# RWKV's normalisation moved from the end of the kernel into the second half of its chain

## The chip, the cores and the metric

The kernel runs on one core of one Trainium2 chip. Times are device microseconds (us) of one execution. A core has TensorE (PE in the rows, its weight loads PEld), VectorE (DVE), ScalarE (ACT), GpSimd (POOL) and SyncE (SP), which issues nearly all DMAs. Each engine works through its own list of instructions in order.

## The reference, cut to what matters

One layer takes 2048 latent and 256 context tokens of width 1024. After a projection one half of the heads does RWKV-7 time mixing in both directions, the other half latent attention:

```
S = S*w + (S@a) b + v k        y = S@r            (forward and backward)
y  = y_f + y_b
yn = (y - mean) * rsqrt(var + 64e-5) * lnx_g + lnx_b        (per head of 64)
rw = (yn + bonus) * silu(gate),   bonus = sum(r*(k_f+k_b)*r_k) * v
mla = softmax(q k^T) v * silu(gate)            (8 heads, 2304 keys)
out = rms_norm(x + gate * (concat(rw, mla) @ w_out))
```

## The kernel before, in words

`phase_in` projects (to about 960 us of the span), `qkv` makes queries, keys and values (to about 1207 us), then `attention` runs. It has 16 jobs (4 pairs of heads, 4 blocks of 512 queries), each of 9 macro steps; a macro step scores two key tiles for two heads (L1425 to L1427, three fp32r products each), exponentiates on ScalarE (L1429), sums the denominators on GpSimd (L1434), and multiplies by V (L1452). Between the scores PE makes the next job's row maxima (L1306), which VectorE reduces (L1307); both share three PSUM banks (`bs`) with the scores.

RWKV works on 36 chunks of 64 tokens, forward and backward at once, and rides along: a chunk n takes three macro steps, called thirds here: m = 0 (`chain1`, `scores` of chunk n+2, `chain1b`), m = 1 (`chain2`), m = 2 (`chain3`, `chain4`, `scores` of n+3). `slot` is called five times in a macro step and gives a stage of the chunkwise inverse (`inverse`, a generator) and `transposed`. `load_bk` issues the load of x and its scaling (L247 to L253). 18 macro steps of the chain run in `qkv`, the next 99 in jobs 0 to 10. `inverse` masks the 128 x 1024 matrix `ph` three times per chunk on VectorE (L343) and spreads results into block-diagonal tiles, one direction by a ScalarE, one by a VectorE copy (L348). `chain4` writes each direction's y to DRAM (L466).

When the chain is done, `post` prepares the output weights and then, for 16 tiles of 128 tokens, loads both y, sums and normalises them on VectorE (L1546 to L1571), transposes on PE (L1578), gates, splits into high and low parts and writes `s_mix`. `out_tiles` loads `s_mix` and multiplies by the weights (L1609), adds the residual and normalises. `late` hands out steps of `post`, and then of `out_tiles`, one quarter of the tokens at a time, between the macro steps. A quarter can start when the last pair of heads is done with it, and in the kernel before only when all of `post` is done.

The order on PE is that of the code; on the other engines a scheduler sets it within the dependencies.

Of the kernel before, what the change touches and what calls it, by code (L numbers as in the profile page):

```python
# [8 lines left out]
F32 = mybir.dt.float32  # L9
# [130 lines left out]
class Rwkv:  # L140
# [3 lines left out]
    def __init__(self, kern, es):  # L144
# [4 lines left out]
        self.total = 3 * (NC + 3)  # L149
# [9 lines left out]
        lvl = st_.tile([P, 4, P], F16, name="lvl")  # L159
# [13 lines left out]
        nc.gpsimd.memset(self.E, 1.0)  # L173
        lo_, up_ = slice(0, 64), slice(64, 128)
# [21 lines left out]
    def slot(self, g):  # L196

        k, j = divmod(g, 5)
        n, m = divmod(k, 3)
        n -= 3  # L200
        if m == 1 and j == 2:
            if 0 <= n + 2 < self.NC:
                self.transposed(n + 2)
            if 0 <= n + 3 < self.NC:
                self.load_bk(n + 3)
        for p in list(self.inv):
            if g - 15 * (p + 1) - 7 in self.STAGES:
                if next(self.inv[p], None) is None:
                    del self.inv[p]

    def tiled(self, k, between=None):
# [5 lines left out]
        if m == 0:  # L217
# [65 lines left out]
    def transposed(self, n):  # L283
# [3 lines left out]
        for d in range(2):  # L287
# [4 lines left out]
            nc.scalar.copy(t, ps)  # L292
# [27 lines left out]
    def inverse(self, n):  # L320
# [20 lines left out]
        def masked(i):  # L341
            pm = op.tile([P, 8, P], F16, name=f"pm{par}")
            nc.vector.tensor_tensor(pm, ph, self.lv8(i), op=ALU.mult)  # L343
            return pm

        def spread(name, x):
            for d, ur, vr in self.dirs:
                (nc.vector.tensor_copy if d else nc.scalar.copy)(self.bd[name][ur, :, ur], x[ur])  # L348
            return self.bd[name]

        pm = masked(0)
        T = None
        yield 1
        for i in range(3):
# [38 lines left out]
        Rf = s["R"] = op.tile([P, 8, 64], F32, name="Rf", bufs=2)  # L393
# [16 lines left out]
    def chain1b(self, n):  # L410
# [11 lines left out]
        if self.full(n):  # L422
            y = s["y"] = self.op.tile([P, 512], F32, name="y")
# [30 lines left out]
    def chain4(self, n):  # L454
# [9 lines left out]
        nc.vector.tensor_tensor(y, ps, y, op=ALU.add)  # L464
        for (d, ur, vr), c in zip(self.dirs, self.chunks[n]):
            nc.sync.dma_start(self.k.s_y[d, c * 64:c * 64 + 64], y[vr])  # L466


class Kern:
# [37 lines left out]
    def load_consts(self):  # L507
# [7 lines left out]
        self.blk = c.tile([P, P], F32, name="blk")  # L515
# [3 lines left out]
    def vectors(self, raw):  # L519
# [4 lines left out]
        self.vec = c.tile([P, NV], F32, name="vec")  # L524
# [711 lines left out]
    def late(self, rest):  # L1236
# [10 lines left out]
        self.pc += (34 + 11 * (L // P)) / (self.POST_T * rest)  # L1247
# [4 lines left out]
    POST_T = 0.75  # L1252
# [3 lines left out]
    RW_QKV = 18  # L1256

# [64 lines left out]
    def attention(self, top, es, right, k, q, load_q, maxima, sets, pieces):  # L1322
# [77 lines left out]
        for ji, (hp, qt) in enumerate(jobs):  # L1400
# [10 lines left out]
            rate = 2 * NQS * NT / max(1, 4 * (NM - 2)) + 8  # L1411
            for m in range(NM):
                if k < rw.total:
                    rw.begin(k)
                elif self.post_ is None:
                    right.close()
# [4 lines left out]
                for j in range(4):  # L1421
# [13 lines left out]
                    if 1 <= m < NM - 1:  # L1435
                        due += rate
# [30 lines left out]
        while k < rw.total:  # L1467
# [4 lines left out]
            k += 1  # L1472
        if self.post_ is None:
# [8 lines left out]
    def post(self, es):  # L1482
# [32 lines left out]

# [5 lines left out]
        h64 = lambda t: t.rearrange("p (h i) -> p h i", i=64)  # L1521
# [15 lines left out]
        V = nc.vector  # L1537
        D1 = []
        nx = load(0)
        for tt in range(NTL + 2):  # L1540
            cur, nx = nx, load(tt + 1)
            if cur:

                ya, vg = cur
                y, y2, vt = h64(ya[:, 0]), h64(ya[:, 1]), h64(vg[:, 0])
                V.tensor_tensor(y, y, y2, op=ALU.add)  # L1546
                yield 1
                st = sp.tile([P, 2, 8], F32, name="st", bufs=3)
# [143 lines left out]
```

## Time and profile before

| | us |
|---|---|
| median of 3 runs (lowest, highest) | 3057.66 (3046.7, 3091.68) |
| profiled execution | 3088.95 |
| its span | 3087.2 |
| PE / DVE / POOL / ACT busy | 2757.4 / 1852.2 / 1407.5 / 1320.9 |
| mean granted TensorE clock | 0.931 |

The page cuts the span into 40 slices of 77 us; jobs 0 to 10 (with the chain) fill slices 17 to 32, jobs 11 to 15 the rest. The clock is given as a share of 2.4 GHz; it has two levels, 1.0 and 0.5 (1.2 GHz), and a value between is a mean over time.

### The profile page before, as it was taken

How to read it: one execution, taken by the hardware profiler on the slowest of the kernel's cores; microseconds unless marked ns; L12 is line 12 of the kernel's file. 1: busy time of each engine (PE TensorE's matmuls, PEld its weight loads, DVE VectorE, ACT ScalarE, POOL GpSimd, SP SyncE). 2: the span in 40 equal slices, each digit the busy share in tenths (PEclk: the TensorE clock that was granted, in tenths of full speed). 3: DMA queues.
4: the chain of work that ended last, by engine and by line, in shares of the span. 5: the costliest groups of instructions: out<-in, count | busy, mean ns of one | idle time of the engine just before them, and what ended most of it. 6: DMA issues, size and time to landing. Idle time of an engine off the chain costs nothing.

```text
span 3087.2 us, 55094 instructions
## 1 busy us (share of the span) xinstructions
PE 2757.4 (89%) x22035; PEld 2081.2 (67%) x22035; DVE 1852.2 (60%) x2867; ACT 1320.9 (43%) x2317; POOL 1407.5 (46%) x1220
## 2 busy tenths in 40 slices
PE   5999999999998898899888888888998977888998
PEld 3997899987787786666666666666666644444776
DVE  3356834266523575777766776775776757997213
ACT  3446744355523433445444444444454442333221
POOL 2323323332332122566555566564665655776332
PEclk7998999999899998999998999998999977898999
DMA  5234542234545776122133222233221144433443
GB/s 195 80 91 125 143 149 88 80 105 121 165 142 174 251 227 157 50 69 70 39 100 89 61 70 60 59 87 88 75 69 49 36 124 128 123 106 116 147 137 116
DMA packets 409466, 336.66 MB, mean 109 GB/s; under 512 B 130598, under 2 KB 341841, under 8 KB 408185
## 3 DMA queue, kind: packets, MB, share of 16 engines
q1 hardware_dynamic: 405775, 327.19, 36.2%
q8 instruction: 173, 2.83, 0.4%
q0 software_dynamic: 992, 3.21, 0.3%
q10 hardware_dynamic: 2442, 2.73, 0.3%
q14 instruction: 84, 0.69, 0.1%
HBM read 210.68 MB, written 122.31 MB: 108 GB/s over the span
## 4 chain that ended last, share of the span: by engine, by line
PE 44%; DVE 14%; DMA 7%; ACT 5%; issue 3%; POOL 1%; SPq 1%; ACTq 0%; POOLq 0%; DVEq 0%
PE bo L1452 7%; PE bx L1609 6%; PE bs L1425 4%; DMA x<-s_x 4%; DVE m L1307 4%; PE pm L117 4%; PE bs L1306 3%; PE bs L1427 3%; PE bs L1426 3%; ACT pt L1429 2%; PE bc L407 2%; PE bx L332 2%; DVE pm L343 2%; DVE x L253 2%; PE bs L1097 2%
## 5 line engine op out<-in xcount | busy, mean ns | idle before, releaser
L1434 POOL TENSOR_TENSOR acc<-acc,pt 128x512 f32<-128x512 f32 x512 | 673.3, 1332 | 612.6 <-ACT pt L1429 608.1
L1429 ACT ACTIVATE pt<-bs 128x512 f32<-128x512 f32 x576 | 342.4, 598 | 574.3 <-PE bs L1427 554.8
L1307 DVE TENSOR_REDUCE m<-bs 128x1 f32<-128x512 f32 (+1 forms) x736 | 401.3, 567 | 187.9 <-PE bs L1306 184.0
L1425 PE MATMUL bs<-q,kt 97*128 97x512 f32 x576 | 282.2, 490 | 44.6 <-ACT pt L1429 22.2
L1452 PE MATMUL bo<-pt,vt 128*64 128x512 f32 x1152 | 310.9, 665 | 0.0
L549 POOL TENSOR_TENSOR wlo<-wraw,whi 128x1024 fp32r<-128x1024 f32 (+1 forms) x56 | 134.3, 2399 | 276.2 <-PE pm L117 177.8
L1427 PE MATMUL bs<-q,kt 97*128 97x512 f32 x576 | 237.9, 413 | 0.0
L1426 PE MATMUL bs<-q,kt 97*128 97x512 f32 x576 | 236.9, 411 | 0.0
L1306 PE MATMUL bs<-kt,q 96*128 96x512 f32 (+1 forms) x480 | 181.9, 408 | 54.3 <-DVE m L1307 18.1
L1425 PEld LDWEIGHTS bs<-q,kt 97*128 97x128 f32 x576 | 112.9, 196 | 125.8 <-ACT pt L1429 39.8
L1306 PEld LDWEIGHTS bs<-kt,q 96*128 96x128 f32 x480 | 91.1, 190 | 120.0 <-ACT pt L1429 43.3
L132 ACT COPY u<-pm 128x342 f32<-128x342 f32 (+1 forms) x168 | 74.1, 441 | 214.7 <-PE pm L117 214.5
L1452 PEld LDWEIGHTS bo<-pt,vt 128*64 128x64 f32 x1152 | 80.3, 153 | 126.8 <-issue 122.1
L1427 PEld LDWEIGHTS bs<-q,kt 97*128 97x128 f32 x576 | 114.1, 198 | 27.3
L1609 PE MATMUL bx<-wohi,big 128*128 128x512 f32 x496 | 126.0, 394 | 3.8 <-DMA big<-s_mix 3.8
L253 DVE TENSOR_TENSOR x<-x 128x512 f32<-128x512 f32 x72 | 65.8, 952 | 99.4 <-ACT x L250 99.3
L1426 PEld LDWEIGHTS bs<-q,kt 97*128 97x128 f32 x576 | 115.1, 200 | 4.6
L978 POOL TENSOR_TENSOR xt<-z,nk 128x512 f32<-128x512 f32 (+1 forms) x40 | 53.1, 1327 | 142.8 <-ACT z L977 80.6
L343 DVE TENSOR_TENSOR pm<-bdph,lvl 128x1024 f16<-128x1024 f16 x108 | 108.0, 1000 | 8.5 <-PE bx L332 5.2
L1609 PEld LDWEIGHTS bx<-wohi,big 128*128 128x128 f32 x496 | 93.7, 190 | 25.0 <-issue 4.8
L1645 DVE TENSOR_TENSOR acc<-bx,big 128x512 f32<-128x512 f32 x32 | 22.0, 690 | 143.3 <-PE bx L1609 137.2
L826 DVE SCALAR_TENSOR_TENSOR kd<-z,u 128x512 f32<-128x512 f32 x32 | 38.9, 1218 | 111.4 <-ACT z L824 111.4
(321 smaller groups left out, 6548.6 us busy)
## 6 DMA issues: line engine op xcount, KB each, us to landing
wraw<-in_w_in SPq DMA_DIRECT2D x54, 512.0 KB
x<-s_x SPq DMA_DIRECT2D x72, 384.0 KB
s_x<-xt SPq DMA_DIRECT2D x32, 512.0 KB
big<-s_mix SPq DMA_DIRECT2D x24, 512.0 KB
s_kn<-hl SPq DMA_DIRECT2D x36, 256.0 KB
ar<-s_nr SPq DMA_DIRECT2D x72, 128.0 KB
uv<-s_v SPq DMA_DIRECT2D x72, 128.0 KB
s_x<-cum SPq DMA_DIRECT2D x32, 256.0 KB
```

Of the source, the lines that this page charges most:

```text
L253: nc.vector.tensor_tensor(self.bk[:, d], self.bk[:, d], cum[:, d].unsqueeze(2).to_broadcast([P, 4, 2, 64]), op=ALU.mult)
L343: nc.vector.tensor_tensor(pm, ph, self.lv8(i), op=ALU.mult)
L549: (eng_lo or nc.vector).tensor_tensor(lo, x, hi.bitcast(F32), op=ALU.subtract)
L1306: nc.tensor.matmul(ps[:, 0:w], q[0:96, e, 0, i * P:(i + 1) * P], ks[e], start=True, stop=True)
L1307: nc.vector.tensor_reduce(m5[:, e * NQS + i, j:j + 1], ps[:, 0:w], axis=AX.X, op=ALU.max)
L1425: nc.tensor.matmul(ps, ks[:, e, 0, sl], q[:, e, 0], start=True, stop=False)
L1426: nc.tensor.matmul(ps, ks[:, e, 0, sl], q[:, e, 1], start=False, stop=False)
L1427: nc.tensor.matmul(ps, ks[:, e, 1, sl], q[:, e, 0], start=False, stop=True)
L1429: nc.scalar.activation(pt, ps, AF.Exp, scale=SCALE)
L1434: nc.gpsimd.tensor_tensor(acc[e], held[e] if kt == 1 else acc[e], pt, op=ALU.add)
L1452: nc.tensor.matmul(oo[64 * e:64 * e + 64], VS[j][:, i, 64 * e:64 * e + 64], pts[kt, e], start=kt == 0, stop=kt == NK - 1)
L1609: nc.tensor.matmul(ps, x[:, i], a[:, k, 512 * h:512 * h + 512], start=n == 0, stop=n == last)
```

## The change

1. `post` loses the RWKV tiles. From chunk `half` = 20 on, where the other direction's y of the same tokens lies in DRAM already, `chain4` starts a generator `normed`: the y of the other direction is loaded (`load_other`), and ten steps, one per slot, do the sum, the normalisation (gain and bias in ScalarE's copy out of PSUM after the transposition), the bonus (GpSimd, transposed too), the gate, the split (low half on GpSimd) and the writes to `s_mix`. Three macro steps are added at the chain's end (`total`). 
2. `inverse` keeps one of its three masks; the other two become a multiplication as the product is spread from PSUM, both directions on VectorE (`level`). Copies of R go to ScalarE. One of two copies in `transposed` goes to VectorE.
3. `load_bk` and `transposed` move from m = 1 to m = 0.
4. The maxima are shared 1.5 : 1 : 0.6 over the thirds in the first half of the chain, evenly after it, and after the chain from the third macro step of a job on.
5. `POST_T` goes from 0.75 to 0.3 with far fewer steps, so that `out_tiles` may start as soon as a quarter is ready, at a lower rate, and waits six steps behind its first load.

```diff
-        self.total = 3 * (NC + 3)
+        self.half = NCC + (NC - NCC) // 2
+        self.total = 3 * (NC + 3) + 3
...
-        if m == 1 and j == 2:
-            if 0 <= n + 2 < self.NC:
-                self.transposed(n + 2)
-            if 0 <= n + 3 < self.NC:
-                self.load_bk(n + 3)
+        if m == 0 and j == 3 and 0 <= n + 2 < self.NC:
+            self.transposed(n + 2)
+        if m != 1 or j == 1:
+            next(self.norm, None)
...
                 self.load_ar(n + 3)
+                self.load_bk(n + 3)
...
                 self.chain2(n)
+                if n >= self.half:
+                    self.load_other(n)
...
-            nc.scalar.copy(t, ps)
+            (nc.vector.tensor_copy if d else nc.scalar.copy)(t, ps)
...
+        def level(name, x, i):
+
+            for d, ur, vr in self.dirs:
+                nc.vector.tensor_tensor(self.bd[name][ur, :, ur], x[ur],
+                                        self.lvl[ur, i, ur].unsqueeze(1).to_broadcast([64, 8, 64]), op=ALU.mult)
...
-                pm = masked(1)
...
-            G = spread(f"g{par}", prod(pm, T))
+            G = level(f"g{par}", prod(ph, T), lev)
...
-                        pm = masked(2)
...
-                        Rb = spread("f", R)
+                        Rb = spread("f", R, both=True)
...
+        if n < self.half:
+            for (d, ur, vr), c in zip(self.dirs, self.chunks[n]):
+                nc.sync.dma_start(self.k.s_y[d, c * 64:c * 64 + 64], y[vr])
+        else:
...
+            self.norm = self.normed(n, s)
...
+            nc.gpsimd.tensor_tensor(h64(vb[vr]), h64(s["uv"][d][vr]), bc(bon[vr, t // P], 64), op=ALU.mult)
+        yield 1
+        V.tensor_tensor(y, y, s["yo"], op=ALU.add)
+        yield 1
...
+        V.tensor_reduce(st[:, 0], h64(y), axis=AX.X, op=ALU.add)
+        V.tensor_scalar(st[:, 0], st[:, 0], 1.0 / 64, None, op0=ALU.mult)
+        yield 1
+        V.tensor_tensor(h64(y), h64(y), bc(st[:, 0], 64), op=ALU.subtract)
+        sq = op.tile([P, 4, 2, 64], F32, name="gt")
+        nc.scalar.activation(flat(sq), y, AF.Square)
+        yield 1
+        V.tensor_reduce(st[:, 1], h64(flat(sq)), axis=AX.X, op=ALU.add)
+        V.tensor_scalar(st[:, 1], st[:, 1], 1.0 / 64, 64e-5, op0=ALU.mult, op1=ALU.add)
+        nc.gpsimd.tensor_tensor(st[:, 0], st[:, 1], self.k.mhalf.to_broadcast([P, 8]), op=ALU.pow)
+        yield 1
+        V.tensor_tensor(h64(y), h64(y), bc(st[:, 0], 64), op=ALU.mult)
...
+        pb = self.k.banks.tile([P, 2, 512], F32, name="bc")
+        for q, x in enumerate((y, vb)):
+            for b in range(4):
+                nc.tensor.transpose(pb[:, q, b * P:(b + 1) * P], x[:, b * P:(b + 1) * P], self.k.ident)
+        for b in range(4):
...
+            nc.scalar.activation(y[:, bs], pb[:, 0, bs], AF.Identity, scale=self.lgb[:, 0, b:b + 1],
...
+        V.tensor_tensor(y, y, pb[:, 1], op=ALU.add)
+        yield 1
+        V.tensor_tensor(y, y, g.rearrange("p b e t -> p (b e t)"), op=ALU.mult)
+        yield 1
...
+        self.k.split(hi, lo, y.rearrange("p (b e t) -> p b e t", e=2, t=64), eng_lo=nc.gpsimd)
+        for q, x in enumerate((hi, lo)):
+            for d, t in enumerate(t0):
+                nc.sync.dma_start(self.k.s_mix[q, 0:4, :, t:t + 64].rearrange("b p t -> p b t"),
...
-    POST_T = 0.75
+    POST_T = 0.3
...
+    MAXIMA = (1.5, 1, 0.6)
...
         nx = self.out_load(qt * nt, nk)
-        yield 1
+        for _ in range(6):
+            yield 1
```

**VectorE at the end of third m = 2 of chunk 25.** `bdg` is the spread product, `st` the state, `y` the output, `sm` the masked scores, `m` the maxima. Before:

```order
L348 CAST bdg_8168<-bx 64x8x64
L370 TENSOR_TENSOR R_22902<-bx,R_22522 128x512
L343 TENSOR_TENSOR pm_23083<-bdph_8160,lvl 128x1024
L348 COPY bdf<-R_22902 64x8x64
L450 TENSOR_TENSOR st_8153<-bx,st_8154 128x512
L452 TENSOR_TENSOR st_8153<-st_8153,gg 128x256 x2
L464 TENSOR_TENSOR y<-bx,y 128x512
L313 TENSOR_TENSOR sm_22955<-bc,mask 128x4x128 x2
```

Now:

```order
L361 TENSOR_TENSOR bdg_8168<-bx,lvl 64x8x64 x2
L384 TENSOR_TENSOR R_22996<-bx,R_22605 128x512
L463 TENSOR_TENSOR st_8153<-bx,st_8154 128x512
L465 TENSOR_TENSOR st_8153<-st_8153,gg 128x256 x2
L477 TENSOR_TENSOR y<-bx,y 128x512
L503 TENSOR_TENSOR y<-y,bt 128x512
L506 TENSOR_REDUCE st<-y 128x8
L507 TENSOR_SCALAR st<-st 128x8
L509 TENSOR_TENSOR y<-y,st 128x512
L325 TENSOR_TENSOR sm_23047<-bc,mask 128x4x128 x2
```

The mask (L343) and the copy of R are gone; four operations of `normed` stand between y and the masked scores.

**PE in macro step 4 of job 13.** `bo` is the product with V. Before:

```order
L1427 MATMUL bs<-q,kt_11432 128x512
L1306 MATMUL bs<-kt_11432,q 128x512 x2
L1425 MATMUL bs<-q,kt_11432 128x512
L1426 MATMUL bs<-q,kt_11432 128x512
L1427 MATMUL bs<-q,kt_11432 128x512
```

Now:

```order
L1508 MATMUL bs<-q,kt_11420 128x512
L1383 MATMUL bs<-kt_11416,q 128x512
L1622 MATMUL bx<-wohi,big 128x512 x6
L1506 MATMUL bs<-q,kt_11420 128x512
L1507 MATMUL bs<-q,kt_11420 128x512
L1508 MATMUL bs<-q,kt_11420 128x512
```

Groups of six output products now stand between the scores from job 13 on. Of the 768 output products, before 549 stood in job 15 up to its last product with V; now 144 stand in job 13, 192 each in job 14 and in job 15 up to there, and 240 behind it.

**SP in the chain's second half.** Before, one chunk:

```order
L281 DMA uv_19906<-s_v 64x512
L281 DMA uv_19907<-s_v 64x512
L466 DMA s_y<-y 64x512 x2
L276 DMA ar<-s_nr 128x512
L274 DMA ar<-s_nr 128x4x64 x2
L247 DMA x<-s_x 128x768 x2
```

Now:

```order
L490 DMA bt<-s_y 64x512 x2
L539 DMA s_mix<-gt 128x4x64 x2
L539 DMA s_mix<-vb 128x4x64 x2
L293 DMA uv_20841<-s_v 64x512
L293 DMA uv_20842<-s_v 64x512
L520 DMA gt<-s_g 128x4x64 x2
L288 DMA ar<-s_nr 128x512
L286 DMA ar<-s_nr 128x4x64 x2
L259 DMA x<-s_x 128x768 x2
```

Two stores become two loads of y, two of the gate and four stores, ahead of the next chunk's loads.

## Rows read from the trace of the kernel before

**Rows 1.** The page, busy tenths and clock tenths in 40 slices.

```profile
DVE  3356834266523575777766776775776757997213
...
PEclk7998999999899998999998999998999977898999
```

**Rows 2.** Stretches (one job each): length; PE, PEld, DVE, ACT, POOL busy; clock, DMA.

```profile
1693.00:1808.00 115.00, 104.28 (x1198) 71.18 (x1198) 81.51 (x124) 55.65 (x100) 72.60 (x68) 0.96 0.23 67
...
2038.00:2170.00 132.00, 114.84 (x1230) 81.32 (x1229) 85.92 (x156) 55.96 (x100) 70.74 (x67) 0.90 0.33 93
...
2495.00:2606.00 111.00, 82.98 (x258) 45.30 (x258) 82.05 (x145) 35.53 (x61) 58.12 (x45) 0.73 0.52 157
...
2606.00:2694.00 88.00, 72.47 (x250) 38.59 (x251) 76.87 (x107) 28.28 (x50) 59.31 (x44) 0.83 0.37 108
...
2694.00:2778.00 84.00, 68.51 (x248) 35.84 (x248) 80.77 (x118) 29.75 (x52) 63.88 (x44) 0.89 0.40 116
...
2778.00:2886.00 108.00, 97.00 (x381) 61.10 (x379) 65.41 (x94) 28.45 (x50) 59.94 (x44) 0.92 0.42 122
...
2886.00:3056.00 170.00, 170.00 (x735) 127.56 (x735) 35.21 (x48) 34.10 (x59) 54.68 (x47) 1.00 0.49 144
...
3056.00:3087.00 31.00, 21.09 (x87) 14.74 (x83) 15.90 (x23) 6.40 (x11) 6.08 (x7) 0.92 0.17 68
```

**Rows 3.** Waits of PE, 2495 to 2843 us: total, times, longest.

```profile
PE bs L1425 <- DVE m L1307: 19.8, 15, 4.0
PE bs L1306 <- DMA q<-s_qr: 13.6, 3, 6.1
```

**Rows 4.** Stretches in job 4: m = 2, m = 0, m = 1, m = 2.

```profile
1716.00:1732.00 16.00, 13.89 (x148) 9.50 (x146) 13.36 (x19) 5.41 (x10) 11.28 (x11) 0.79 0.07 23
...
1732.00:1744.00 12.00, 11.47 (x137) 8.02 (x135) 7.72 (x13) 3.37 (x6) 6.19 (x5) 1.00 0.11 26
...
1744.00:1756.00 12.00, 10.67 (x119) 6.93 (x116) 6.49 (x10) 8.80 (x16) 5.03 (x4) 1.00 0.33 102
...
1756.00:1771.00 15.00, 12.07 (x164) 8.15 (x159) 13.74 (x20) 5.91 (x11) 11.47 (x12) 1.00 0.05 14
```

**Rows 5.** Groups by line in job 15: count, busy us, mean ns, idle before.

```profile
L1609 PE MATMUL bx<-wohi,big 128*128 128x512 f32 x370 | 93.1, 391 | 0.0
...
L1609 PE MATMUL bx<-wolo,big 128*128 128x512 f32 x179 | 45.6, 390 | 0.0
```

**Rows 6.** The chain of waits: start, us, what.

```profile
2858.89 5.46 PE bx L1609 x24
...
1344.67 4.75 DMA x<-s_x
```

**Rows 7.** Groups by line and shape, jobs 1 to 9.

```profile
L343 DVE TENSOR_TENSOR pm<-bdph,lvl 128x1024 f16<-128x1024 f16 x81 | 85.6, 1057 | 1.0 <-PE bx L332 0.7 <-ACT bdph L317 0.3
...
L348 DVE COPY bdf<-R 64x512 f16<-64x512 f16 x27 | 23.2, 860 | 0.8
...
L370 DVE TENSOR_TENSOR R<-bx,D 128x512 f16<-128x512 f32 x81 | 55.4, 684 | 12.4 <-PE bx L332 12.3
...
L290 PEld LDWEIGHTS bc<-ident,x 128*128 128x128 f32 x216 | 24.2, 140 | 26.1 <-ACT tr L292 24.7
...
L380 POOL TENSOR_TENSOR bdg<-sm,bdph 64x512 f16<-64x512 f32 x55 | 68.2, 1240 | 4.9 <-PE bx L332 2.8
```

**Rows 8.** Groups by line and shape, 2494 to 2850 us.

```profile
L1567 DVE TENSOR_TENSOR big<-big,st 128x512 f32<-128x512 f32 x16 | 17.5, 1097 | 6.4 <-POOL st L1564 6.4
...
L1580 DVE TENSOR_TENSOR big<-bx,acc 128x512 f32<-128x512 f32 x16 | 10.9, 678 | 0.0
...
L1549 DVE TENSOR_REDUCE st<-big 128x8 f32<-128x512 f32 x16 | 10.8, 674 | 0.0
...
L1558 DVE TENSOR_SCALAR st<-st 128x8 f32<-128x8 f32 x16 | 9.4, 587 | 0.0
```

**Rows 9.** One line: nanoseconds, least, median, most.

```profile
L1571 DVE TENSOR_TENSOR big<-big,acc x16: 677/692/1754, 2588.1 to 2830.9; 128x512 f32<-128x512 f32 x16
```

More of the change, by code (lines that the diff above doesn't have):

```diff
@@ L158, in __init__ @@
         nc.sync.dma_start(self.mask, kern.I["mask"])
-        lvl = st_.tile([P, 4, P], F16, name="lvl")
+        lvl = self.lvl = st_.tile([P, 4, P], F16, name="lvl")
         nc.sync.dma_start(lvl, kern.I["lvl"])
@@ L173, in __init__ @@
         nc.gpsimd.memset(self.E, 1.0)
+        self.lgb = st_.tile([P, 2, 4], F32, name="lgb")
+        nc.sync.dma_start(self.lgb[:, 0], kern.I["rw_lnx_g"][0].rearrange("(b p) -> p b", p=P))
+        nc.sync.dma_start(self.lgb[:, 1], kern.I["rw_lnx_b"][0].rearrange("(b p) -> p b", p=P))
+        bonx = st_.tile([P, kern.L // P, 8], F32, name="bonx")
+        nc.sync.dma_start(bonx[0:64], kern.bon[64:128])
+        nc.sync.dma_start(bonx[64:128], kern.bon[0:64])
+        self.bon = (bonx, kern.bon)
+        self.norm = iter(())
         lo_, up_ = slice(0, 64), slice(64, 128)
@@ L339, in packed, with spread @@
             return op.tile([P, 8, 64], F16, name=f"{name}{par}", bufs=bufs)
[L341 to L346, printed above, removed]
+        def spread(name, x, both=None):
             for d, ur, vr in self.dirs:
-                (nc.vector.tensor_copy if d else nc.scalar.copy)(self.bd[name][ur, :, ur], x[ur])
+                (nc.vector.tensor_copy if d and not both else nc.scalar.copy)(self.bd[name][ur, :, ur], x[ur])
             return self.bd[name]
-        pm = masked(0)
+        def level(name, x, i):
+            for d, ur, vr in self.dirs:
+                nc.vector.tensor_tensor(self.bd[name][ur, :, ur], x[ur],
+                                        self.lvl[ur, i, ur].unsqueeze(1).to_broadcast([64, 8, 64]), op=ALU.mult)
+            return self.bd[name]
+        pm = op.tile([P, 8, P], F16, name=f"pm{par}")
+        nc.vector.tensor_tensor(pm, ph, self.lv8(0), op=ALU.mult)
         T = None
@@ L392, in inverse @@
         ps = prod(Fb, R)
-        Rf = s["R"] = op.tile([P, 8, 64], F32, name="Rf", bufs=2)
+        Rf = s["R"] = op.tile([P, 8, 64], F32, name="Rf")
         nc.vector.tensor_tensor(Rf, ps, R, op=ALU.add)
@@ L422, in chain1b @@
         if self.full(n):
-            y = s["y"] = self.op.tile([P, 512], F32, name="y")
+            y = s["y"] = self.op.tile([P, 512], F32, name="y", bufs=2)
             for d, ur, vr in self.dirs:
@@ L464, in chain4, with load_other @@
         nc.vector.tensor_tensor(y, ps, y, op=ALU.add)
-        for (d, ur, vr), c in zip(self.dirs, self.chunks[n]):
-            nc.sync.dma_start(self.k.s_y[d, c * 64:c * 64 + 64], y[vr])
+        if n < self.half:
+            for (d, ur, vr), c in zip(self.dirs, self.chunks[n]):
+                nc.sync.dma_start(self.k.s_y[d, c * 64:c * 64 + 64], y[vr])
+        else:
+            for _ in self.norm:
+                pass
+            self.norm = self.normed(n, s)
+    def load_other(self, n):
+        o = self.S[n]["yo"] = flat(self.op.tile([P, 2, 4, 64], F32, name="bt"))
+        for (d, ur, vr), c in zip(self.dirs, self.chunks[n]):
+            self.nc.sync.dma_start(o[vr], self.k.s_y[1 - d, c * 64:c * 64 + 64])
@@ L1246, in late @@
             return
-        self.pc += (34 + 11 * (L // P)) / (self.POST_T * rest)
+        self.pc += 34 / (self.POST_T * rest)
         while self.pc >= 1:
@@ L1409, in attention @@
             due = 0.0
-            rate = 2 * NQS * NT / max(1, 4 * (NM - 2)) + 8
+            share = [1 if k + i >= rw.total and i > 1 else self.MAXIMA[(k + i) % 3] if k + i < 3 * (rw.half + 3) else
+                     1 if k + i < rw.total else 0 for i in range(1, NM - 1)]
+            rate = [0] + [2 * NQS * NT * x / (4 * sum(share)) + 8 for x in share] + [0]
             for m in range(NM):
@@ L1415, in attention @@
                 elif self.post_ is None:
+                    for _ in rw.norm:
+                        pass
                     right.close()
@@ L1435, in attention @@
                     if 1 <= m < NM - 1:
-                        due += rate
+                        due += rate[m]
                         while due > 0:
@@ L1472, in attention @@
             k += 1
+        for _ in rw.norm:
+            pass
         if self.post_ is None:
```

89 lines of the change are left out of this document (22 added, 67 removed).

## The prediction

> **What bounds the kernel now.** I read the slices of the page first. VectorE is at 7 tenths while the chain runs, and the clock line has its lowest digit of the whole attention, 7, in the 33rd and 34th slices, where jobs without the chain begin; the last slices are PE's alone [rows 1]. So I cut the time by jobs. Job 4 stands for those with the chain: PE busy 104.28 of 115.00 us, VectorE 81.51, ScalarE 55.65, GpSimd 72.60, clock 0.96. Job 7, where the pair of heads changes and keys are loaded afresh, takes 132 us [rows 2]. Jobs 11 to 13 should be the short ones, since the chain is over, but take 111, 88 and 84 us with the clock at 0.73, 0.83 and 0.89. In jobs 12 and 13 VectorE is busy 76.87 of 88 and 80.77 of 84 us, with the tiles of `post`: it bounds them. Job 15 is the opposite: PE 170.00 of 170.00 us at full clock, because nearly all output products wait for `post` and fall there [rows 2]. PE's waits in 2495 to 2843 us name VectorE's maxima (19.8 us at L1425) and, at three starts of jobs, the load of q (13.6 us) [rows 3]. Four stretches of job 4 show how the chain's time lies over its thirds: m = 2 takes 16 and 15 us with VectorE busy 13.36 and 13.74, m = 0 and m = 1 take 12 each with VectorE at 7.72 and 6.49 [rows 4]. In m = 2, then, VectorE is late; elsewhere PE sets the time.
>
> **The end, 2495 to 3087 us, 592 us now.** The change takes the tiles of `post` off VectorE here and spreads the output products. What remains is PE's own work. An output product costs 5.46/24 = 0.2275 us [rows 6]. Job 15 holds 370 + 179 = 549 of them [rows 5], 125 us, so its nine macro steps of attention take the other 170 - 125 = 45 us, 5.0 each. Five jobs make 225 us; maxima in four of them, some 40 products of 512 columns or as much, at the same price, 36; 768 output products 175; five sums of denominators about 1 us each, 5; the end behind PE, 31 - 21 = 10 us [rows 2]. Sum 451, a floor. On it I put what won't vanish: PE idle for a tenth, as in job 4, in the 2.3 jobs that have no output products between the scores (12 us); the fresh keys in job 11, as much as job 7 has over job 4 (17); the load of q at three starts, which comes behind the last read of the old q as before (13.6, so 14); and the lower clock after such gaps, 5 us at each of three (15), an estimate from jobs 12 to 14, where it is below 1.0. That makes 509, a gain of **83 us**. Bounds: the floor (141) and twice the losses (25). GpSimd and ScalarE don't bind: in the busiest of these jobs they have 63.88 and 35.53 us. The longer drain, 240 products behind the last product with V, is PE work that only changes place, and counts in the 175.
>
> **The chain's first half, in jobs 0 to 5, 17 chunks.** Per chunk VectorE loses two masks of 1.057 us and one copy of 0.860, and gains two spreads, priced as the nearest operation of one PSUM source (0.684), and the copy of `transposed`, taken alike [rows 7]: 2.97 less, 2.05 more, so only 0.9 us in all. But both masks and the copy stood in m = 2. There it loses 2.97 and gains one spread, 0.68; and of some 5.5 maxima 2.5 go elsewhere, about 0.68 each. 13.5 us of VectorE become about 9.5, and m = 2 falls to PE's own time: 12.07 us busy at clock 1.00 in the second of the two stretches [rows 4], 12.5 with small gaps, 3 less than now. m = 0 takes up maxima, spread and copy and gives back about 1. So 2 us per chunk, **34 us**; bounds 0 (all given back in m = 0) and 3 x 17 = 51. Moving `load_bk` changes which wait VectorE meets at x: the load takes 4.75 us [rows 6] and is now issued behind three loads of ar at the end of m = 0. I give it nothing; VectorE's masks and maxima of m = 0 cover it, and without that cover it would cost what it costs now. `transposed` is the same eight products in another third, and the four chain chunks in `qkv`, the moved constants and ScalarE's copies (it is half idle) I cost at nothing.
>
> **The second half, 16 chunks.** Each gains `normed`. On VectorE that is four operations with both sources in SBUF (1.097 each), one from PSUM (0.678), two reductions (0.674) and two small ones (0.587) [rows 8]: 7.6 us. VectorE had 81.51/3 = 27.2 us per chunk of 38.3 and gets 27.2 - 0.9 + 7.6 = 33.9: not over PE's time, but as dense everywhere as m = 2 is now. PE gains eight transpositions of 0.14 [rows 7], 1.1 us. GpSimd gains three passes of 1.24 [rows 7] and a power, some 5 us on 24; ScalarE gains a square, four pieces and a cast and loses three copies. The order shows four operations of `normed` between y and the masked scores at the end of m = 2, some 4 us; behind them PE's first maxima and ScalarE's square wait. They roughly fill what the mask and copy leave. I take 2 us per chunk: **32 us lost**. Bounds: PE's 1.1 us alone (18), and 5.5 us, when all three thirds are late as m = 2 is now (88).
>
> Sum: 83 + 34 - 32 = 85 us gained, 3089 - 85 = 3004 in terms of the profiled execution. That one is 31 us above the median of 3057.66, so the forecast for the median is **2973**. Own range of this case: 2940 to 3005.
>
> **Rivals.** *The second half costs nothing extra.* VectorE has 11 us per chunk free in m = 0 and m = 1, and `normed` is spread over slots. Then it loses PE's 18 us, the first half gains 45 and the end 108 (half the losses named above): 135 gained, 2923. For it: the even spread. Against it: VectorE works in order, and the multiplication by the power waits for GpSimd.
>
> *VectorE bounds the second half.* Operations with two SBUF sources stretch when GpSimd works: L1571 takes 0.692 in the median and 1.754 at most [rows 9], while the one from PSUM has a mean of 0.678 and the reduction 0.674 [rows 8]. If the four in `normed` all take the most, they add 4 x (1.75 - 1.10) = 2.6 us to the 33.9, and the multiplications for x and the state stretch likewise; VectorE then has no gap left and each chunk is 5.5 us longer. 88 lost, the end gains 75, the first half 20: 7 gained, 3051, no change. For it: GpSimd is at 63% in the chain now and goes to about 75%. The Trainium skill (SBUF — State Buffer, "Who interferes with whom") says that a VectorE instruction with two SBUF inputs and a GpSimd instruction that reads SBUF exclude each other, the later one blocked for the whole of the first; by that rule this case is the result, and the row's 1.754 agrees with it, as 0.692 plus one pass of GpSimd's.
>
> *Slower.* `vb`, the low half, has one buffer. GpSimd's bonus product of the next chunk waits until the low half's store has landed, and that store stands as third and fourth of four on SP. At 4.75 us for a landing [rows 6], plus SP's four issues, less the 2.5 us of two subtractions that stand between [rows 7], GpSimd stands still for about 4 us per chunk, with the denominators queued behind. Three buffers of each `pt` absorb some 4 us. If the landing takes 8 us more, ScalarE's exponentials wait for GpSimd, PE for them, and the clock falls: 12 us per chunk, 192 lost, against 75 and 20 gained: 97 slower, 3155. It decides against the kernel from 95/16 = 6 us per chunk, and makes it measurably slower from (95 + 61)/16 = 9.8. Against it: DMA engines are at 0.23 in job 4 [rows 2]. The Trainium skill (DMA: Bandwidth & Descriptors, "Specifications") puts the least transfer for line rate at 512 B, and the new stores write pieces of 256 B; no run here shows such a store into `s_mix`.
>
> That the change doesn't do what it says is out: the order has the output products in jobs 13 to 15.
>
> **Chances and range.** Forecast 0.52, nothing extra 0.24, VectorE bounds 0.16, slower 0.08. A measurement of this kernel can tell 2%, 61 us, from no change, so faster means below 2997, which holds in about three quarters of the forecast's case and in all of the first rival's: 0.63. Slower, above 3119: 0.07. The rest, 0.30, is no change. The range 2905 to 3050 takes in the first rival with some room and the forecast whole, up to the edge of the VectorE case.
>
> **What the profile will show.** The end right: jobs 11 to 13 of 60 to 95 us with the clock above 0.9 and VectorE well under 70% busy, 85 us less from macro step 99 on. The first half right: m = 2 steps of 12 to 13 us at full clock; wrong if m = 0 grows by more than 2. The second half: chunks of 40 to 41 us against 38 to 39; VectorE rows of `normed` with means near 1.1 and idle time before them under 1 us each. If GpSimd waits for `s_mix` before the bonus product, or ScalarE's exponential for GpSimd's sum, the slow rival is at work. The forecast is wrong if jobs 12 and 13 stay over 80 us without output products, or the chunks from 20 on take over 43 us.

## The result and the profile after

The changed kernel takes 3103.1 us in the median of four runs (3093.02 to 3120.97), the kernel before 3065.33 in the same comparison (3046.7 to 3091.68): 1.0122 times as long, 95% interval 1.0076 to 1.0168. It is slower by 1.2%, within the 2% called no change; the forecast was 2973 us, with a range of 2905 to 3050.

In the profiled executions (3105.35 us, span 3103.6; before 3088.95 and 3087.2) the 16.4 us between the spans split by stages, from the first score product of each job. (The medians lie 37.8 us apart: the kernel before was profiled 23.6 us above its median, the change 2.3 above its own.)

| us | before | change | difference | forecast |
|---|---|---|---|---|
| start of job 0 | 1208.2 | 1198.1 | -10.1 | 0 |
| jobs 0 to 5 | 715.9 | 718.7 | +2.8 | -34 |
| jobs 6 to 10 | 570.7 | 655.1 | +84.4 | +32 |
| job 11 to the end | 592.4 | 531.7 | -60.7 | -83 |

The page of the change answers [rows 1]. VectorE no longer has its 9s in slices 35 and 36:

```profile
DVE  3256834266534575676666677776677775533313
...
PEclk8998999999999997999988999998898898899999
```

The stretches answer [rows 2], with the same columns (length; PE, PEld, DVE, ACT, POOL busy; clock, DMA share, GB/s): jobs 4, 7, 8, 11, 12, 15 and what follows the last product with V.

```profile
1685.80:1800.00 114.20, 100.73 (x1199) 68.57 (x1198) 80.81 (x125) 52.98 (x94) 69.07 (x67) 1.00 0.22 66
2045.90:2201.70 155.80, 126.76 (x1257) 90.59 (x1256) 107.60 (x187) 61.03 (x113) 88.58 (x80) 0.84 0.36 99
2201.70:2333.50 131.80, 114.55 (x1223) 78.85 (x1222) 95.79 (x147) 59.66 (x111) 84.31 (x77) 0.90 0.26 72
2571.90:2677.40 105.50, 79.11 (x269) 44.03 (x268) 64.15 (x117) 35.55 (x63) 59.04 (x47) 0.78 0.47 131
2677.40:2746.20 68.80, 62.08 (x226) 33.13 (x225) 27.79 (x45) 23.23 (x40) 47.38 (x39) 0.92 0.08 23
...
2945.90:3034.90 89.00, 89.00 (x380) 60.80 (x380) 15.70 (x20) 28.00 (x49) 50.10 (x41) 1.00 0.34 104
3034.90:3103.60 68.70, 57.46 (x246) 44.40 (x242) 24.61 (x34) 7.63 (x14) 7.16 (x9) 0.96 0.41 130
```

The end does what was said: job 12 falls from 88 to 69 us, job 15 from 170 to 89. Jobs with `normed` (7 and 8) are 156 and 132 us long. VectorE is busy 95.79 of 131.80 us in job 8, 73%: fuller, not full. PE is idle there for 17 us and has the clock at 0.90.

Three stretches of job 4 answer [rows 4]: m = 2, m = 0, m = 1.

```profile
1711.05:1723.22 12.17, 10.43 (x147) 7.28 (x144) 7.90 (x13) 5.37 (x9) 7.29 (x7) 1.00 0.07 16
1723.22:1738.37 15.15, 13.43 (x150) 9.52 (x148) 9.91 (x16) 4.18 (x7) 6.26 (x5) 1.00 0.14 37
1738.37:1750.26 11.89, 10.01 (x112) 6.19 (x108) 8.69 (x13) 7.60 (x14) 8.24 (x10) 1.00 0.30 93
```

m = 2 fell from 16 and 15 us to 12, at full clock, as forecast; m = 0 rose from 12 to 15 and took it all back. The means over jobs 1 to 5, cut at the first score product of each macro step, say the same: m = 2 falls from 15.46 to 12.15 us, m = 0 grows from 11.87 to 15.08.

### The profile page after: what moved, and what is told of

It is laid out like the page before. It is cut to its first block, busy times and chain, and to the rows that moved or that the text cites. A ratio compares the mean times of both kernels' runs of the same rounds, so it can differ in the third digit from the quotient of the medians.

```text
span 3103.6 us, 55266 instructions
## 1 busy us (share of the span) xinstructions
PE 2751.6 (89%) x22099; PEld 2086.7 (67%) x22099; DVE 1792.8 (58%) x2803; ACT 1311.7 (42%) x2309; POOL 1430.8 (46%) x1268
## 4 chain that ended last, share of the span: by engine, by line
PE 45%; DVE 13%; ACT 5%; DMA 4%; issue 4%; POOL 2%; SPq 1%; ACTq 0%; POOLq 0%; DVEq 0%
PE bo L1533 7%; PE bx L1622 5%; PE bs L1506 5%; PE pm L117 4%; PE bs L1383 3%; PE bs L1508 3%; PE bs L1507 3%; DVE m L1384 3%; ACT pt L1510 2%; PE bx L344 2%; PE bc L420 2%; DMA x<-s_x 2%; DVE bdg L361 2%; DVE x L265 2%; PE bs L1172 1%
## 5 line engine op out<-in xcount | busy, mean ns | idle before, releaser
L1515 POOL TENSOR_TENSOR acc<-acc,pt 128x512 f32<-128x512 f32 x512 | 656.3, 1296 | 558.7 <-ACT pt L1510 551.7
L624 POOL TENSOR_TENSOR wlo<-wraw,whi 128x1024 fp32r<-128x1024 f32 (+1 forms) x56 | 134.8, 2407 | 276.4 <-PE pm L117 175.6
L344 PEld LDWEIGHTS <-bdg 128*128 128x128 f16 x1728 | 70.8, 101 | 57.1 <-issue 54.7
L384 DVE TENSOR_TENSOR R<-bx,R 128x512 f16<-128x512 f32 x108 | 73.7, 682 | 49.3 <-PE bx L344 48.1
L361 DVE TENSOR_TENSOR bdg<-bx,lvl 64x512 f16<-64x512 f32 x144 | 98.6, 685 | 4.6 <-PE bx L344 2.4
```

Source lines behind the costliest of these rows:

```text
L344: nc.tensor.matmul(ps[:, h], lhsT[:, h], r, start=plus is None, stop=also is None and (plus is None or h == 7))
L361: nc.vector.tensor_tensor(self.bd[name][ur, :, ur], x[ur], self.lvl[ur, i, ur].unsqueeze(1).to_broadcast([64, 8, 64]), op=ALU.mult)
L624: (eng_lo or nc.vector).tensor_tensor(lo, x, hi.bitcast(F32), op=ALU.subtract)
L1515: nc.gpsimd.tensor_tensor(acc[e], held[e] if kt == 1 else acc[e], pt, op=ALU.add)
```

## The experiments

Ratios are to the kernel before, in the same comparison, with 95% intervals; stages are from each kernel's profiled execution, cut as above. A stage is uncertain by some 10 us: jobs 0 to 5 have the same code in the change, 4 and 7 and take 718.7, 714.4 and 710.3 us; in 3 they have that of before but for the number of buffers, and take 704.5 against 715.9.

| | median us | ratio | jobs 0 to 5 | 6 to 10 | 11 to end |
|---|---|---|---|---|---|
| before | | 1 | 715.9 | 570.7 | 592.4 |
| change | 3103.1 | 1.0122 [1.0076, 1.0168] | 718.7 | 655.1 | 531.7 |
| 1 no normalisation | 3090.28 | 1.0074 [1.0049, 1.0099] | 721.4 | 573.8 | 601.3 |
| 2 inverse alone | 3035.11 | 0.9890 [0.9863, 0.9917] | 682.2 | 553.0 | 591.9 |
| 3 normalisation alone | 3100.76 | 1.0108 [1.0071, 1.0145] | 704.6 | 667.5 | 529.7 |
| 4 no power | 3080.55 | 1.0067 [1.0030, 1.0103] | 714.4 | 646.7 | 518.9 |
| 5 inverse, new places | 3079.68 | 1.0032 [1.0001, 1.0062] | 718.6 | 574.5 | 582.8 |
| 6 inverse, new shares | 3031.17 | 0.9882 [0.9821, 0.9942] | 689.7 | 558.6 | 587.3 |
| 7 no VectorE work | 3057.2 | 0.9954 [0.9922, 0.9985] | 710.3 | 609.7 | 528.7 |
| 8 leaner `post` | 3073.6 | 1.0024 [0.9991, 1.0058] | 684.4 | 556.5 | 632.6 |
| 9 change, old places | 3057.46 | 0.9981 [0.9963, 1.0000] | 684.6 | 643.1 | 526.3 |
| 10 and products in m = 1 | 3045.31 | 0.9941 [0.9910, 0.9971] | 691.1 | 625.8 | 526.3 |
| 11 inverse, `transposed` | 3070.93 | 1.0023 [1.0000, 1.0046] | 717.3 | 569.4 | 595.1 |
| 12 half of the tiles | 3037.64 | 0.9925 [0.9895, 0.9955] | 690.8 | 583.2 | 572.6 |

### Which part costs: 1, 2 and 3

1: the change without `normed`; `post` and `late` as before.

```
-        self.half = NCC + (NC - NCC) // 2
-        self.total = 3 * (NC + 3) + 3
+        self.half = NC
+        self.total = 3 * (NC + 3)
```

> The changed kernel with the normalisation back where it was: the tiles of post, its share POST_T and its rates as before, the chain without its three added macro steps; the inverse, the moved loads and the shares of the maxima stay as changed, the shares now over the whole chain. Theory A (the second half's 84 us are the normalisation's own): jobs 6 to 10 take what jobs 0 to 4 take in the changed kernel, 114 to 136 us each and 92 for the last, some 570 in all; the end is that of before; total 3040 to 3065 us, same as before. Theory B (the moved loads and the new spreads are late in the second half for a reason of their own): jobs 6 to 10 stay above 620 us and the total is about 3100.

2: the kernel before with the new `inverse` (`level`, `spread` of R on ScalarE, one `Rf`) and nothing else.

```
-            G = spread(f"g{par}", prod(pm, T))
+            G = level(f"g{par}", prod(ph, T), lev)
```

> The kernel before with the new inverse alone (one mask, two spreads with the mask on VectorE, copies of R on ScalarE, one buffer for Rf). Theory A (masks and copy made m = 2 late): m = 2 macro steps fall from 13.6 to 16 us to 12 to 13, m = 0 and m = 1 stay, 2 us per chunk over 33 chunks, total 2990 to 3010 us. Theory B (PE waits in m = 2 for a bank that the spread holds, and two spreads behind one another on VectorE hold it longer than a copy on each of two engines): m = 2 falls by less than 1 us, total 3040 to 3070.

3: the change with the old `inverse`, places and even shares.

```
-    MAXIMA = (1.5, 1, 0.6)
+    MAXIMA = (1, 1, 1)
...
-            G = level(f"g{par}", prod(ph, T), lev)
+            G = spread(f"g{par}", prod(pm, T))
```

> The changed kernel with the old inverse (its Rf in one buffer), transposed and the loads of x in m = 1 as before, both copies of transposed on ScalarE, and even shares of the maxima; the normalisation in the chain's second half and the early output products stay. Theory A (the loss of the second half is the normalisation's own, and the masks come on top): jobs 6 to 10 take 655 to 680 us, jobs 0 to 5 as before (716), the end as changed; total 3090 to 3120. Theory B (normalisation and moved loads together crowd m = 0): jobs 6 to 10 take 600 to 630 us and the total is 3040 to 3060.

Without normalisation jobs 6 to 10 fall by 81 us, so the second half's loss is its own, as theory A had it (3 says the same: 667.5). The inverse alone gains 33.7 us in jobs 0 to 5, the 34 of the forecast, and is faster than both kernels, though its total lies between the two theories. That it meets the 34 so closely is partly luck: against the 704.5 us of 3, which has the old inverse, the gain is 22. In 1 theory A's total was missed, 3090 us against 3040 to 3065: there is no normalisation in it, yet jobs 0 to 5 take 721 us. Something else of the change eats the inverse's gain.

### The first half: 5, 6 and 11

5: 2 with the new places. 11: 2 with `transposed` moved alone. 6: 2 with the new shares.

```
-        if m == 1 and j == 2:
-            if 0 <= n + 2 < self.NC:
-                self.transposed(n + 2)
+        if m == 0 and j == 3 and 0 <= n + 2 < self.NC:
+            self.transposed(n + 2)
...
-                        due += rate
+                        due += rate[m]
```

(The last two lines belong to 6; in 5 `load_bk` goes to the end of m = 0 and one copy to VectorE too.)

> The kernel before, with the new inverse (as in the run with the inverse alone, 3035 us, job 4 109.4 us) and, added, the new places of `transposed` (m = 0, its second copy on VectorE) and of `load_bk` (end of m = 0). Job 4 of the changed kernel is 114.2 us, 4.8 more than with the inverse alone. Theory P (the new places cost it): job 4 at 112 to 114 us, m = 0 steps 1 to 2.5 us longer than 12.1, total 3050 to 3070. Theory S (the new shares of the maxima cost it): job 4 at 109 to 110, total 3030 to 3040.

> The kernel before, with the new inverse and, added, the shares 1.5, 1 and 0.6 of the maxima over m = 0, 1 and 2 while the chain runs. Theory S (the shares give back in m = 0 what m = 2 gains): job 4 at 112 to 114 us, m = 0 at 14 to 15, total 3050 to 3070. Theory P (the new places of the products and the load do): m = 2 falls to about 12 and m = 0 grows by less, job 4 at 107 to 110, total 3020 to 3040.

> The inverse alone (3035 us) with `transposed` moved to m = 0 and nothing else; `load_bk` stays in m = 1. Theory P (the eight products and the wait between their halves cost PE 1.8 us in m = 0, and m = 1 gets no shorter): total 3070 to 3085, m = 0 at 13. Rival (the later load of x costs it): total 3030 to 3045.

By the medians theory P holds in 6 and 11; 5, at 3080 us, lies above both of its ranges. `transposed` alone gives back 35.1 us in jobs 0 to 5 (682.2 to 717.3), and its ratio goes from 0.9890 to 1.0023, some 41 us. What the load and the copy add is not clear of the noise (1.0032 in 5), and the shares cost nothing (0.9882 in 6). PE in m = 0 of job 4, experiment 11 (start, us, what, idle before):

```profile
1720.55 0.60 PE L289 MATMUL bc<-ident,x 128*128 128x128 f32 x4
1721.83 0.65 PE L289 MATMUL bc<-ident,x 128*128 128x128 f32 x4 [0.68 <-ACT tr L291]
```

From 1720.55 to 1722.32 us, the next product's start, 1.77 us go to eight products and a wait for ScalarE between their halves. In m = 1 the same piece takes as long (1713.29 to 1715.06 us in experiment 2), but m = 1 hardly gets shorter without it. Stretches m = 0, m = 1, m = 2 of job 4, experiment 2:

```profile
1695.99:1708.12 12.13, 11.60 (x140) 8.19 (x138) 7.95 (x13) 3.49 (x6) 6.19 (x5) 1.00 0.20 50
1708.12:1720.26 12.14, 10.81 (x120) 7.07 (x117) 7.13 (x11) 8.82 (x16) 5.43 (x6) 1.00 0.31 92
1720.26:1733.99 13.73, 11.21 (x151) 7.84 (x147) 11.26 (x18) 5.48 (x10) 10.61 (x11) 1.00 0.06 20
```

and of experiment 11:

```profile
1714.83:1728.71 13.88, 12.67 (x148) 9.15 (x146) 8.04 (x13) 4.67 (x8) 6.23 (x5) 1.00 0.13 33
1728.71:1741.73 13.02, 9.96 (x112) 6.14 (x109) 9.83 (x13) 7.60 (x14) 8.71 (x10) 1.00 0.27 86
1741.73:1759.22 17.49, 15.41 (x151) 11.04 (x148) 9.96 (x16) 5.37 (x9) 7.36 (x6) 0.71 0.06 16
```

m = 0 grows by 1.75 us. m = 1 has 0.85 us less of PE and still doesn't get shorter: VectorE's share of it rises from 7.13 to 9.83 us, and PE's waits in jobs 1 to 5 name `Rf` for 7.3 us, which experiment 2 doesn't have. m = 2 here has the clock at 0.71, which is not typical. In the mean of jobs 1 to 5 m = 0 grows by 2.04 us (11.61 to 13.65), m = 1 falls by 0.33 and m = 2 grows by 0.48, with the clock at 0.91 there instead of 0.98. That the scaling of x, freed earlier, is what moved into m = 1 fits the 2.7 us, but was not tried alone.

### The second half: 4, 7, 9 and 10

4 leaves out GpSimd's power, 7 the power and all VectorE operations of `normed` (in both half of the output is then not RWKV's). 9 is the change with the old places; 10 is 9 with the eight transpositions of `normed` in m = 1.

```
-        if m != 1 or j == 1:
+        if (m, j) in self.NORM:
             next(self.norm, None)
+    NORM = ((0, 0), (0, 1), (0, 2), (0, 3), (0, 4), (1, 1), (1, 4), (2, 0), (2, 1), (2, 2))
```

> The changed kernel without GpSimd's power in the normalisation (VectorE multiplies by the variance itself; the inverse root is left out). Theory A (VectorE stands 25.6 us before the multiplication that waits for GpSimd's power, in order, and PE behind it): the 16 waits go, and with them PE's waits for R and part of the low clock; jobs 6 to 10 fall by 30 to 45 us, total 3055 to 3075. Theory B (VectorE's work itself, 7 us per chunk, makes the second half late): under 12 us, total 3090 to 3100.

> The changed kernel without the nine VectorE operations of `normed` and GpSimd's power (left out, so that half of the output is not RWKV's); the loads, GpSimd's bonus product, ScalarE's square and pieces, the eight transpositions, the split and the stores stay. Theory V (VectorE's volume makes the second half dear): jobs 6 to 10 fall from 655 us to 585 to 600, total 3025 to 3045. Rival (what the other engines and queues got makes it dear): jobs 6 to 10 stay above 630, total above 3065.

> The changed kernel with `transposed` and `load_bk` back in m = 1 (both copies on ScalarE). The places alone cost 3080 - 3035 = 45 us when they were added to the inverse. Theory P (m = 0 is PE's and takes 1.8 us per chunk for the eight products and the copy between them, while m = 1 has a wait for ScalarE that hides them): m = 0 falls by about 1.8 us, 36 chunks, total 3050 to 3065. Rival (the normalisation fills m = 1 in the second half, so the old place is no longer free there): only the first half gains, total 3075 to 3090.

> The run with the old places, and the eight transpositions of `normed` in m = 1 instead of m = 2; by the order its sum with the bonus and its product with the gate then stand on VectorE ahead of m = 2's maxima and spreads. Theory Q (the loss comes from work put ahead of the spread of the product on VectorE, for which `chain3` waits on PE): m = 2 of the second half falls by 2 to 3 us, total 25 to 45 below the run with the old places alone. Theory V (VectorE's and PE's volume): what m = 2 gains m = 1 loses, total within 10 us of that run.

Where the 81 us lie, two stretches tell, jobs 6 to 10 of experiment 1 and of the change (columns as above):

```profile
1914.30:2488.20 573.90, 508.68 (x5764) 343.80 (x5762) 378.79 (x612) 252.88 (x449) 329.83 (x308) 0.97 0.23 64
```

```profile
1916.80:2571.90 655.10, 559.48 (x5884) 385.05 (x5882) 484.22 (x749) 290.11 (x539) 413.01 (x365) 0.90 0.26 73
```

PE is idle for 30 us more (95.6 against 65.2) and busy for 51 more. The eight transpositions in each of 15 chunks are 13 us of these (0.87 us each time, as counted further down); the other 38 go with the lower clock, 0.90 against 0.97.

7 falls between its theories (3057; jobs 6 to 10 at 609.7): VectorE's work and the power make 45 of the 81 us, and without them PE's wait for R inside the inverse is 1.4 us instead of the 18.4 shown below. The other 36 stay with what 7 leaves in, transpositions, loads, stores and the parts on GpSimd and ScalarE, and were not taken apart. In 4 the power, for which VectorE waits 25.6 us in 15 chunks, is only 8 of them, no more than a stage is uncertain by; the median, 3081, lies between its theories. 9 lands where its theory put it (3057), though the second half gains just 12 us from it and the first 34, the rival's split.

10 lies 12 us below 9 in the median and 17 in the stage, between the 25 that theory Q wanted at least and the 10 that theory V allowed. PE's waits in the second half (total us, times, longest) tell why it is a gain. The change, 1917 to 2571 us:

```profile
PE bx L460 <- DVE bdg L361: 20.6, 13, 2.2
PE bx L344 <- DVE R L384: 18.4, 14, 1.9
...
PE bs L1383 <- DVE m L1384: 7.1, 14, 1.6
```

Experiment 2, 1881 to 2434 us:

```profile
PE bx L448 <- DVE bdg L349: 20.8, 13, 2.2
...
PE bs L1307 <- DVE m L1308: 3.4, 10, 0.4
...
PE bx L332 <- DVE R L372: 1.7, 6, 0.4
```

Experiment 9, 1881 to 2524 us:

```profile
PE bx L346 <- DVE R L386: 19.3, 15, 2.5
PE bs L1385 <- DVE m L1386: 11.3, 14, 2.1
```

Experiment 10, 1893 to 2519 us:

```profile
PE bx L464 <- DVE bdg L365: 20.5, 13, 2.2
PE bs L1387 <- DVE m L1388: 12.7, 13, 2.1
...
PE bx L348 <- DVE R L388: 5.7, 11, 1.6
```

The wait for `bdg` is the same in all of them (20.4 in 9). The one for R, inside the inverse, is what `normed` adds: 18.4 us against 1.7. From 9 to 10, with the work out of m = 2, it falls from 19.3 to 5.7, and the maxima come hardly later (12.7 against 11.3). VectorE in m = 2 of job 8, the change (idle before it in brackets):

```profile
2280.39 0.68 DVE L531 TENSOR_TENSOR y<-y,bc 128x512 f32<-128x512 f32 x1
...
2282.24 1.50 DVE L533 TENSOR_TENSOR y<-y,gt 128x512 f32<-128x512 f32 x1
2283.67 0.68 DVE L384 TENSOR_TENSOR R<-bx,R 128x512 f16<-128x512 f32 x1
2284.27 1.27 DVE L1384 TENSOR_REDUCE m<-bs 128x1 f32<-128x512 f32 x2
2285.46 1.38 DVE L361 TENSOR_TENSOR bdg<-bx,lvl 64x512 f16<-64x512 f32 x2
```

and PE behind it:

```profile
2284.40 0.39 PE L344 MATMUL bx<-R,bdg 128*128 128x64 f16 x8 [1.27 <-DVE R L384]
2286.99 1.98 PE L460 MATMUL bx<-uv,tr 128*64 128x64 f32 x32 [2.20 <-DVE bdg L361]
```

The sum with the bonus and the product with the gate stand in VectorE's list ahead of R and the spread, and PE waits for those. m = 2 of job 8 in experiment 9:

```profile
2226.44:2245.31 18.87, 14.68 (x159) 10.64 (x155) 15.83 (x24) 8.39 (x16) 15.01 (x15) 0.82 0.22 56
```

and in experiment 10:

```profile
2229.09:2243.56 14.47, 11.15 (x151) 7.84 (x147) 12.87 (x19) 6.32 (x11) 14.32 (x15) 1.00 0.23 56
```

4.4 us less in this stretch, of which PE busy 3.5. Over jobs 6, 8 and 9 m = 2 falls from 17.3 to 14.1 us in the mean, as theory Q had it; m = 0 and m = 1 together rise by 1.9, so more than half of it is lost again, as theory V had it.

### The end: 8 and 12

8 is 2 with tiles that take less of VectorE: bonus and low half on GpSimd, gain and bias in ScalarE's pieces.

```
-                V.tensor_tensor(vt, vt, bc(self.bon[:, tt], 64), op=ALU.mult)
+                nc.gpsimd.tensor_tensor(vt, vt, bc(self.bon[:, tt], 64), op=ALU.mult)
...
-                self.split(hl[:, 0], hl[:, 1], mx)
+                self.split(hl[:, 0], hl[:, 1], mx, eng_lo=nc.gpsimd)
```

> The inverse alone (3035 us) with tiles of `post` after the chain as before, but leaner on VectorE: the bonus product and the low half go to GpSimd, gain and bias into ScalarE's Identity behind the transposition, and bonus is transposed too; some 11 us of VectorE per tile become 7, on 16 tiles, and PE gets 64 transpositions (9 us). Theory V (VectorE's volume bounds jobs 12 and 13, where it is busy 77 of 88 and 81 of 84 us): those jobs fall to 65 to 75 us each, total 2990 to 3020. Rival (the tiles' chain of waits, now through GpSimd and ScalarE, bounds them): total 3030 to 3045.

12 is 10 with eight of the tiles left to `post`.

```
-        self.half = NCC + (NC - NCC) // 2
+        self.half = NCC + 3 * (NC - NCC) // 4
...
+        tiles = range(L // P // 4, 3 * L // P // 4)
```

> The run with the transpositions in m = 1 (3045 us), but only chunks 28 to 35 are normalised in the chain; the other eight tiles are left to `post` behind the chain as before (POST_T 0.45). In the chain eight chunks give back 4.2 us each (jobs 6 to 10: 626 us against 559 with the inverse alone, for 16 chunks): 33 us less. Theory A (behind the chain the tiles cost their VectorE time, since jobs 11 and 12 have little room: 88 us on 65 of 101 and 28 of 68 us): the end grows by 25 to 30, total 3035 to 3050. Rival R (the tiles fit into the waits of jobs 11 and 12, and only moving all 16 was too much): the end grows by 0 to 12, total 3010 to 3025, below both the kernel before and the inverse alone.

Both theories on 8 miss, the rival in its size: the total, 3074 us, lies above both ranges, and the end is 41 us longer than in 2. Jobs 12 and 13 of experiment 8:

```profile
2563.60:2664.90 101.30, 74.28 (x266) 40.49 (x265) 72.31 (x96) 36.21 (x71) 73.17 (x56) 0.82 0.37 106
2664.90:2760.40 95.50, 72.84 (x267) 40.59 (x266) 63.06 (x91) 35.75 (x70) 70.39 (x55) 0.82 0.35 100
```

VectorE has room now, 63.06 of 95.50 us, and the jobs are longer (87 and 85 in 2). PE's longest wait in these two jobs, 2563 to 2760 us, is for the load of q:

```profile
PE bs L1307 <- DMA q<-s_qr: 29.4, 3, 11.3
```

and VectorE's, in the same stretch, for GpSimd's power:

```profile
DVE big L1566 <- POOL st L1564: 24.6, 10, 3.9
```

What holds up the load of q there was not followed further. 12 gives 43 us of the second half back, 10 more than expected, and loses 46 behind the chain, more than the 25 to 30 of theory A; the median, 3038, is in theory A's range because the two misses cancel. Splitting the tiles gains nothing over the inverse alone.

## Why the prediction was wrong

The median lies 130 us above the forecast. 101 of them are in the stages below, where the profiled executions are compared (3105.35 us against 3004). The other 29 are in the prediction's last step: it took off 31 us because the kernel before had been profiled that far above the median of its first three runs, while the changed kernel was profiled 2 us above its own. That step carried an accident of one execution into the forecast.

**The first half** (34 forecast, -3 measured). The working on VectorE and m = 2 held: the inverse alone gives 33.7, or 22 against experiment 3. The step that failed is "`transposed` is the same eight products in another third, [...] I cost at nothing". It moved from a third where PE has slack into one that [rows 4] show as PE's own (11.47 of 12.00 us busy), and its 1.77 us there are hardly given back in m = 1: of the 36.5 us by which the change stands behind the inverse alone in jobs 0 to 5, `transposed` alone makes 35. The bound of 0, "all given back in m = 0", was the case, by a price that I had not counted; m = 0 grew by more than 2 us, the sign that the prediction had named.

**The second half** (32 forecast, 84 measured). 5.6 us instead of 2 for each of the 15 chunks in these jobs (the sixteenth is normalised in job 11), at the bound of 5.5 taken from three late thirds; a chunk takes 655.1/15 = 43.7 us, over the 43 that the prediction had named as a sign against it. The work was sized well: the means of `normed` in 15 chunks are

```profile
L533 DVE TENSOR_TENSOR y<-y,gt 128x512 f32<-128x512 f32 x15 | 19.7, 1312 | 0.2
L517 DVE TENSOR_TENSOR y<-y,st 128x512 f32<-128x512 f32 x15 | 19.5, 1298 | 25.6 <-POOL st L515 25.6
L503 DVE TENSOR_TENSOR y<-y,bt 128x512 f32<-128x512 f32 x15 | 14.1, 939 | 0.5
L509 DVE TENSOR_TENSOR y<-y,st 128x512 f32<-128x512 f32 x15 | 10.4, 692 | 0.5
```

4.24 us for the four operations with two sources in SBUF, where I had 4 x 1.097 = 4.39 [rows 8]. What failed is "they roughly fill what the mask and copy leave": I added volumes, but work that stands ahead of the operation that PE waits for delays PE, whatever the third has left: the wait for R goes from 1.7 us to 18.4, and back to 1.4 in 7 and 5.7 in 10. I also left out what becomes of the clock, which is the larger part, 38 of the 81 us. From job 8 before (2170 to 2285 us, 104.53 busy of 115.30, clock 0.96) to after (114.55 of 131.80, 0.90), 10 us of the 16.5 are PE busy, and eight transpositions in each of three chunks make 3 x 0.87 = 2.6 of them (from 2277.46 us, where they begin in m = 2 of that job, to 2278.33, where the next product does); the other 7 come with the lower clock. The order in VectorE's list is shown to be a part of the loss (17 us from 9 to 10), not all of it: the 36 us that 7 leaves stay open.

The rival "VectorE bounds the second half" (0.16) had the size, 5.5 us per chunk. Its sum, 3051, is 52 us too low, as far off as the slow rival's 3155 on the other side. Its mechanism is shown only in part: not all four operations take the most (4.24 us, not 7.0), and VectorE is 73% busy. The rule of the Trainium skill that was weighed there (SBUF — State Buffer, "Who interferes with whom") is borne out by the rows: L531, with one source in PSUM, has a mean of 681 ns over the same 15 chunks, L533, with two in SBUF, 1312. The trace shows it operation by operation:

```profile
2260.64 1.15 POOL L400 TENSOR_TENSOR im<-lvl,T 128x512 f16<-128x512 f16 x1
2260.70 1.63 DVE L517 TENSOR_TENSOR y<-y,st 128x512 f32<-128x512 f32 x1 [1.17 <-POOL st L515]
```

VectorE's operation begins 0.06 us after GpSimd's and ends 0.54 us after it. Of the 64 executions of these four lines 27 began with no GpSimd operation running and took 0.69 us each; 37 began while one ran, and each of them ended 0.55 us after that one, however long that still took. The longest, 1.76 us, is so a whole GpSimd operation of 1.26 us and half a microsecond behind it, where the prediction had read 0.692 and one pass. L517 meets one in 10 of 16 chunks, because it waits for GpSimd's power and GpSimd goes straight on to its next operation. L533 meets one every time, and it is the one that stands ahead of the R that PE waits for.

The slow rival is out: GpSimd waits for the store of `vb` 4.5 us in all, 9 times.

**The end** (83 forecast, 60.7 measured). Of the 22 us short job 11 has 18: by my terms 45 + 9 + 1 + 5 + 17 + 5 + 5 = 87 us, measured 105.50, at clock 0.78. PE's waits in it:

```profile
PE bs L1506 <- DVE m L1384: 6.6, 4, 5.3
PE bs L1383 <- DMA q<-s_qr: 5.9, 1, 5.9
PE bs L1383 <- DVE wolo L624: 3.2, 1, 3.2
```

The load of q I had sized as an average over three starts of jobs, the output weights (L624, 16 subtractions on VectorE from 2623.1 to 2666.4 us, in this job) at nothing. How much of the 18 us each of them makes, or the clock, is not settled; some of it is this one execution's, since job 11 takes 103.2, 99.8 and 100.7 us in 3, 9 and 10.

That leaves 10 us of gain ahead of job 0, costed at nothing. It is not settled whose they are: job 0 starts at 1198.5 us in experiment 2, but with the same inverse at 1207.8 in 8, and with the old inverse at 1199.8 in 3; it may be no more than the spread between executions.

One sum of the prediction is off: half of the losses named for the end (12, 17, 14 and 15 us) is 29, so in the first rival the end gains 112 and not 108. Nothing rests on it.

## What to carry to other kernels

Moving work between stages is free only where the target stage is bound by something else: ask for each third which engine sets it, and price the moved piece, its inner waits included, if it is the one. Work on a half-idle engine costs by its place in that engine's list too, not by its volume alone; look for the operation that the bounding engine waits for, and keep additions behind it. When a change bundles several edits, measure them singly: here one of them, the inverse alone, is 1.1% faster (0.989 [0.9863, 0.9917]), with the new shares 1.2% (0.9882 [0.9821, 0.9942]), and the bundle is slower by as much.

## What the runs showed of the hardware

The clock does not follow from the length of a single wait. In experiment 2 `chain3` starts behind a wait of 2.21 us in job 4 and runs at full clock, 32 products in 1.15 us:

```profile
1729.17 1.15 PE L448 MATMUL bx<-uv,tr 128*64 128x64 f32 x32 [2.21 <-DVE bdg L349]
```

In job 8 of the change the same product, behind 2.20 us, takes 1.98 (shown above): PE had stood for another 1.27 us shortly before. That need not be the reason: of the eight waits of 2.2 us in experiment 2 four were followed by a mean clock of 1.00 in the next 3 us, four by 0.52 to 0.69. VectorE's smallest operation was stretched as well, the multiplication of 128x8 numbers:

```profile
L507 DVE TENSOR_SCALAR st<-st x16: 171/176/1424, 1918.8 to 2572.5; 128x8 f32<-128x8 f32 x16
```

(least, median, most, in ns). Of the 16 five took over 0.2 us; in each of these a GpSimd operation was running when it began, and each ended 0.03 us after the end of one.
